# A list schedule of its own that pins the order of every engine's instructions in a two-layer encoder kernel

## The chip, the cores and the metric

The kernel runs as one program on one core of a Trainium2 chip. The metric is device time in microseconds (us), the median of three runs. A core has five engines that each take their instructions strictly in the order in which they were built: PE (matrix products), DVE (vector work), ACT (pointwise functions and casts), POOL (a second, slower vector engine) and SP (here the queue that issues all DMAs). An instruction waits on semaphores for what other engines must have done first, and everything behind it on its engine waits with it.

## The reference

Two layers over one sequence of 512 tokens, width 1024, 16 heads of 64, gated channel mixer of width 2816, all in float32:

```
layer 0: a = rmsnorm(h); q,k,v = split(a @ sb_w_qkv)
         o = stick_breaking_attention(q,k,v)     # sigmoid weights times a running product of (1-beta)
         h = h + rmsnorm(o @ sb_w_o)
         h = h + rmsnorm(conv_ffn(rmsnorm(h)))   # up, causal conv of width 3, gelu(gate)*up, down
layer 1: k,v,f from rmsnorm(h) @ w_kvf; q = rmsnorm(h) @ fox_w_q
         o = softmax(q k/8 + fcum[t] - fcum[s], causal) v
         h = h + rmsnorm(o @ fox_w_o)
         h = h + rmsnorm(conv_ffn(rmsnorm(h)))
```

## The kernel before

**Products.** Each float32 operand is split into a rounded part and a rest (hi and lo), and each product is made of three matmuls: hi·hi, hi·lo and lo·hi. Activations stand transposed in `AH`/`AL`; weights come as 192-odd tiles of 512 KB through a stream: `make` (L129) issues the DMA of a tile into `raw` (two buffers), casts it on ACT to `whi` (L144) and takes the rest on DVE to `wlo` (L148, two halves; three tiles of each output projection on POOL; with a gain folded in, L138/L139). `whi`/`wlo` have eight buffers each, so eight tiles at most are ahead of PE.

**Stages.** A stage `pre` (norm, transposes), `attn0` (16 heads of stick-breaking attention in eight pairs), `ffn0` (output projection, norm, up, down), `attn1` (16 heads of forgetting attention) and `ffn1`.

**A head** (`head`, L411). PE makes the scores of four query blocks (L419) into three PSUM banks. In layer 0: ACT exp (L452), DVE min and mask (L453, L429, L431), ACT ln (L455), DVE scan (L456), ACT exp (L457), DVE product (L458). In layer 1: DVE mask and maximum (L429, L431, L438), ACT exp of four blocks with row sums (L439), DVE reciprocal (L443), scaling of one block on DVE and three on POOL (L446). Then PE transposes the weights (L466), ACT and DVE split them (L472, L473), PE multiplies with V (L478), ACT and DVE take the result out (L487, L488). The next pair's projections (L213, L399) and, for the last heads, the output projection (L521) are what PE can do meanwhile.

**A transition** (`out_proj`, L530, and `mixed`, L576). For each of the four token blocks b the output projection runs over k = 0..7 (L521). Then `post_steps` and `pre_steps`: ACT square and sum (L250), POOL two small instructions for the root (L219, L220), DVE product with the gain and residual sum (L251, L253), again square (L230), root, scaling (L235), then PE transposes of that block (L238), ACT and DVE into `AH`/`AL` (L240, L241). The up projection of the first three chunks runs in two halves of 256 tokens (L605 to L609), so that its first half needs blocks 0 and 1 only.

**What sets the order.** The framework's scheduler orders each engine by a timeline of its own; `tc.high_priority()` marks the norm steps (L225, L245); `out_proj` writes the order of its 32 units out by hand, with `FILL` units between the last heads' parts, and ties each to the one before (`tc.issue_after`, L547); `down_proj` ties its last units the same way, and activation tables are loaded behind the users of the last one (L196).

Of the kernel before, what the change touches and what calls it, by code (L numbers as in the profile page):

```python
# [14 lines left out]
P = 128  # L15
# [13 lines left out]
EARLY = 3  # L29
POOL_ROWS = (1, 5, 7)  # L30
FILL = (4, 5)
# [6 lines left out]
def f32(ap):  # L38
    return ap.bitcast(F32)


@with_exitstack
def tile_trunk(
# [23 lines left out]

    const = ctx.enter_context(tc.tile_pool(name="const", bufs=1))
    small = ctx.enter_context(tc.tile_pool(name="small", bufs=4))
    wp = ctx.enter_context(tc.tile_pool(name="wp", bufs=1))  # L70
# [58 lines left out]
    def make(i):  # L129
# [5 lines left out]
        if g is not None:  # L135
            for k in range(nk):
                s = gcol[:, g + k : g + k + 1]
                nc.scalar.activation(hi[:, k], raw[:, k], AF.Copy, scale=s)  # L138
                nc.vector.scalar_tensor_tensor(  # L139
                    out=lo[:, k], in0=raw[:, k], scalar=s, in1=f32(hi[:, k]), op0=ALU.mult, op1=ALU.subtract  # L140
                )
            made[i] = (hi, lo)
# [48 lines left out]
    users = []  # L191

    def ins(i):
        return getattr(i, "ins", i)

    def act_table(name):  # L196
        with ExitStack() as stack:
            for i in users[-8:]:
                stack.enter_context(tc.issue_after(i))
            ld = nc.scalar.preload_act_table_set(name)  # L200
        return tc.issue_after(ins(ld))

    def uses_table(i):
        users.append(ins(i))
# [18 lines left out]
    def pre_block(b, g, t4, junk):  # L223

        with tc.high_priority():  # L225
            pre_steps(b, g, t4, junk)

    def pre_steps(b, g, t4, junk):
# [52 lines left out]
    class Attn:  # L281
# [128 lines left out]
        def head(self, p, hh):  # L410
# [22 lines left out]
            if fox:  # L433
                masked(z, mask_b, ALU.add)
                st = small.tile([P, 12], F32, name="st")
                for b in (3, 2, 0, 1):
                    sl = slice(ZOFF[b], ZOFF[b] + (b + 1) * P)
                    nc.vector.reduce_max(st[:, b : b + 1], z[:, sl], axis=AX.X, negate=True)  # L438
                    i = nc.scalar.activation(  # L439
                        E[:, sl], z[:, sl], AF.Exp, bias=st[:, b : b + 1], accum_out=st[:, 4 + b : 5 + b]  # L440
                    )
                    uses_table(i)
# [6 lines left out]
            else:  # L449
# [7 lines left out]
                uses_table(nc.scalar.activation(C, C, AF.Exp, scale=-1.0))  # L457
# [3 lines left out]
            for js in ((0,), (1, 3), (2,)):  # L461
                zt = bank("zt")
                o = 0
                for j in js:
                    for b in range(j, NB):
                        tr = nc.tensor.transpose(  # L466
# [22 lines left out]
            return ins(tr), ins(mm)  # L489

        def run(self):
# [7 lines left out]
            for p in range(NPAIR):  # L499
# [3 lines left out]
                end = self.head(p, 1)  # L503
# [7 lines left out]
            return end  # L511


    def unit(b, k, n, a, w, cols=(0, 1)):
# [4 lines left out]
        for i, (s, m) in enumerate(((ah, hi), (ah, lo), (al, hi))):  # L519
            for c in cols:  # L520
                mm = nc.tensor.matmul(  # L521
# [3 lines left out]
        return ins(mm)  # L525
# [4 lines left out]
    def out_proj(done, heads_end):  # L530

        w = {}
        after = []
        one = [(1, k) for k in range(KT)]
        order = [(0, k) for k in range(KT - 2)] + one[: FILL[0]] + [(0, KT - 2), heads_end[0]]
        order += one[FILL[0] : FILL[1]] + [heads_end[1]] + one[FILL[1] :]
        order += [(0, KT - 1)] + [(b, k) for b in (2, 3) for k in range(KT)]
        for step in order:
            if not isinstance(step, tuple):
                after.append(step)  # L540
                continue
            b, k = step
            if k not in w:
                w[k] = take()
            with ExitStack() as stack:
                for i in after:
                    stack.enter_context(tc.issue_after(i))  # L547
                after = [unit(b, k, KT, (AH[:, k, :], AL[:, k, :]), w[k])]
            if k == KT - 1:
                done(b)  # L550

    def down_proj(lhs, done, final, last=4):
        held = []
        for k in range(NC):
# [5 lines left out]
            for b in (0, 2, 3, 1):  # L560
                end = unit(b, k, NC, a, w)
        for b in range(NB):
            for cols in ((0,), (1,)) if final and b == NB - 1 else ((0, 1),):
                with tc.issue_after(end):
                    for k, a, w in held:
# [153 lines left out]
```

## Time and profile before

| | |
|---|---|
| median of 3 runs | 1271.66 us (1269.28 to 1274.44) |
| the profiled execution | 1273.83 us, span of its instructions 1272.1 us |
| PE / DVE / ACT / POOL busy | 97% / 64% / 51% / 8% of the span |
| instructions | 16,820 |

A busy PE is not PE at its best: matmuls overlap, so a row's mean duration (391 ns for 512 columns) is longer than the distance from one start to the next. Groups of instructions show busy time, mean duration of one, and the idle time just before them with what ended it; windows show each engine's busy time in a stretch, and the clock that PE was granted (1.00 is the upper of its two levels).

### The profile page before, as it was taken

Reading aid. Unit: us, or ns where it says so; the run is one execution under the profiler, and the core shown is the slowest. Engines: PE = TensorE matmul, PEld = TensorE weight load, DVE = VectorE, ACT = ScalarE, POOL = GpSimd, SP = SyncE. Lnnn points to the kernel's source line nnn. Section 1 sums busy time; section 2 is a strip of 40 time slices with the busy share of each in tenths; the row PEclk is TensorE's granted clock in tenths of the full one; section 3 lists DMA queues with packets and bytes.
Section 4 is the critical chain, followed back from the end, with each engine's and each line's share of the span. In section 5 each row is a group of like instructions: output and inputs, shape, how many; then the busy total and the mean of one; then the engine's idle time right before and its main releaser. Section 6 shows DMA issues by size and latency. Waiting matters only on the chain. (4 is left out here: it accounts for less than half of the span.)

```text
span 1272.1 us, 16820 instructions
## 1 busy us (share of the span) xinstructions
PE 1232.7 (97%) x6485; PEld 1060.8 (83%) x6485; DVE 811.1 (64%) x1304; ACT 644.6 (51%) x1085; POOL 102.0 (8%) x163
## 2 busy tenths in 40 slices
PE   6999998999999999999999999999999999999998
PEld 6888886789888888888888988978898888888886
DVE  6899898676655555433488887774775555554323
ACT  5767677445433333322488787663454333333221
POOL 1000003020000000000012213341100000000001
PEclk9999999999999999999999999999999999999999
DMA  7421212034333333233233122110543333322311
GB/s 218 136 66 51 67 50 67 23 94 138 111 99 99 97 92 95 98 99 100 67 83 86 53 81 67 58 43 33 149 118 99 99 99 100 97 91 94 99 34 66
DMA packets 145928, 111.97 MB, mean 88 GB/s; under 512 B 4680, under 2 KB 136120, under 8 KB 145848
## 3 DMA queue, kind: packets, MB, share of 16 engines
q1 hardware_dynamic: 145848, 110.90, 28.9%
q8 instruction: 51, 0.84, 0.3%
q14 instruction: 29, 0.24, 0.1%
HBM read 108.79 MB, written 2.10 MB: 87 GB/s over the span
## 5 line engine op out<-in xcount | busy, mean ns | idle before, releaser
L213 PE MATMUL PS<-AH,whi 128*128 128x512 f32 (+1 forms) x1088 | 398.1, 366 | 3.9 <-DVE QS L370 2.6
L213 PE MATMUL PS<-AL,whi 128*128 128x512 f32 (+1 forms) x1088 | 397.2, 365 | 0.0
L213 PE MATMUL PS<-AH,wlo 128*128 128x512 f32 (+1 forms) x1088 | 397.1, 365 | 0.0
L148 DVE TENSOR_TENSOR wlo<-raw,whi 128x512 fp32r<-128x512 f32 x332 | 217.4, 696 | 212.2 <-ACT whi L144 211.7
L144 ACT CAST whi<-raw 128x1024 fp32r<-128x1024 f32 x172 | 180.9, 1052 | 224.7 <-PE PS L213 178.5
L213 PEld LDWEIGHTS PS<-AH,whi 128*128 128x128 f32 x1088 | 205.5, 189 | 36.6 <-DVE QS L370 3.3
L213 PEld LDWEIGHTS PS<-AH,wlo 128*128 128x128 f32 x1088 | 205.3, 189 | 32.0
L213 PEld LDWEIGHTS PS<-AL,whi 128*128 128x128 f32 x1088 | 205.4, 189 | 31.3
L597 DVE SCALAR_TENSOR_TENSOR hc<-PS,cw,hc 128x511 f32<-128x511 f32 (+1 forms) x176 | 130.7, 745 | 2.7
L521 PE MATMUL PS<-whi,al 128*128 128x512 f32 x352 | 109.4, 389 | 0.0
L521 PE MATMUL PS<-wlo,ah 128*128 128x512 f32 x352 | 109.4, 389 | 0.0
L521 PE MATMUL PS<-whi,ah 128*128 128x512 f32 x352 | 109.3, 389 | 0.0
L620 DVE TENSOR_TENSOR al<-act,ah 128x512 fp32r<-128x512 f32 x44 | 30.4, 690 | 117.2 <-ACT ah L619 117.2
L619 ACT CAST ah<-act 128x512 fp32r<-128x512 f32 x44 | 27.4, 623 | 144.8 <-PE PS L521 138.3
L219 POOL TENSOR_SCALAR ss<-ss 128x1 f32<-128x1 f32 x31 | 12.0, 388 | 822.4 <-ACT junk L250 757.1
L399 PE MATMUL PS<-whi,AH 128*128 128x256 f32 x256 | 74.1, 290 | 3.9 <-DVE QS L370 1.6
L521 PEld LDWEIGHTS PS<-wlo,ah 128*128 128x128 f32 x352 | 66.1, 188 | 13.8
L521 PEld LDWEIGHTS PS<-whi,al 128*128 128x128 f32 x352 | 66.1, 188 | 13.7
L521 PEld LDWEIGHTS PS<-whi,ah 128*128 128x128 f32 x352 | 66.1, 188 | 13.6
L399 PE MATMUL PS<-wlo,AH 128*128 128x256 f32 x256 | 74.0, 289 | 0.0
L399 PE MATMUL PS<-whi,AL 128*128 128x256 f32 x256 | 73.6, 288 | 0.0
L602 ACT ACTIVATE hc<-hc 128x512 f32<-128x512 f32 x44 | 27.8, 631 | 86.4 <-DVE hc L597 86.4
(130 smaller groups left out, 1767.5 us busy)
## 6 DMA issues: line engine op xcount, KB each, us to landing
raw<-w_up_dram SPq DMA_DIRECT2D x88, 512.0 KB
raw<-w_down_dram SPq DMA_DIRECT2D x44, 512.0 KB
raw<-sb_w_qkv_dram SPq DMA_DIRECT2D x24, 512.0 KB
raw<-w_kvf_dram SPq DMA_DIRECT2D x16, 512.0 KB
raw<-sb_w_o_dram SPq DMA_DIRECT2D x8, 512.0 KB
raw<-fox_w_q_dram SPq DMA_DIRECT2D x8, 512.0 KB
raw<-fox_w_o_dram SPq DMA_DIRECT2D x8, 512.0 KB
H<-x_dram SPq DMA_DIRECT2D x4, 512.0 KB
```

What stands on the lines that cost most here:

```text
L144: nc.scalar.copy(hi, raw)
L148: eng.tensor_tensor(out=fl[:, s], in0=fr[:, s], in1=fh[:, s], op=ALU.subtract)
L213: nc.tensor.matmul(ps, a[:, k, :m], b[:, k, t0:t1], start=i == 0, stop=i == n - 1)
L219: nc.gpsimd.tensor_scalar(ss[:, 2:3], ss[:, 0:1], 1.0 / D, EPS, op0=ALU.mult, op1=ALU.add)
L399: nc.tensor.matmul(ps[:, o], a[:, k, sl], m[:, k % 4, :], start=i == 0, stop=i == 3 * KT - 1)
L521: mm = nc.tensor.matmul(y[:, c, :], s[:, sl], m[:, 0, c * 512 : (c + 1) * 512], start=k == 0 and i == 0, stop=k == n - 1 and i == 2,)
L597: nc.vector.scalar_tensor_tensor(out=hc[:, s:], in0=y[:, i, : T - s], scalar=col[:, 2 - s : 3 - s], in1=hc[:, s:], op0=ALU.mult, op1=ALU.add,)
L602: uses_table(nc.scalar.activation(hs[0], hs[0], AF.Gelu_apprx_tanh))
L619: nc.scalar.copy(ah, act[:, k, :])
L620: nc.vector.tensor_tensor(out=al, in0=act[:, k, :], in1=f32(ah), op=ALU.subtract)
```

## The change

The kernel records its instructions in program order, as before, and at the end `Order.pin` builds a dependency graph of the whole program (by 64-byte pieces of tiles, PSUM banks, tile buffers, activation tables), gives every instruction a cost by engine, operation and columns, and runs a list schedule: whichever engine is free first takes, among its instructions that are ready, the one of lowest rank. The rank is the place in the program, plus 300 for the split of a weight tile (`BEHIND`), minus 150 for an instruction other than PE's that reads or writes PSUM (`AHEAD`). The order that comes out is then tied on PE, DVE, ACT and POOL by a chain of dependencies from each instruction to the next. The hand-written order of `out_proj`, the high priorities, the ties of `down_proj` and of the table loads go. No instruction is added, removed or changed: 6,485 matmuls and 224 DMAs before and after. The order of the DMAs on SP is not pinned and differs in a few places.

```
+BEHIND = 300
+AHEAD = 150
-FILL = (4, 5)
+class Order:
+    ISSUE, FLIGHT, BYTES = 520, 2100, 200.0
+    HOP = 60
...
+    def cost(self, i):
...
+        if e == "PE":
+            return {512: 227, 384: 171, 256: 120}.get(n, max(109, 0.4427 * n)), 170 + 0.4427 * n
...
+        reads = [x for x in aps if self.columns(x) >= P]
+        narrow = len(reads) < len(aps)
+        n = max([n] + [self.columns(x) for x in reads])
+        if e == "DVE":
+            if n == ZLEN and op == "TensorScalarPtr" and len(reads) == 2:
+                d = 130 + 2.1 * n
+            elif len(reads) > 1 or any(x.bass_ap.tensor.name in self.banks for x in reads):
+                d = 155 + 1.04 * n + 65 * narrow
+            else:
+                d = 150 + 0.53 * n + 60 * narrow
+            return d - 80, d
+        if e == "Activation":
+            d = 135 + 0.9 * n + 150 * narrow + 60 * (len(i.outs) > 1)
+            return d + 20, d
+        if n < P:
+            d = 550 if op == "TensorTensor" else 190
+        else:
+            d = 200 + (2.3 if len(reads) > 1 else 1.3) * n
+        return d, d
...
+    def pin(self, psum, tables):
...
+        start = self.schedule(prog, preds)
+        by = {}
+        for n in sorted(range(N), key=lambda n: (start[n], n)):
+            by.setdefault(self.engine(prog[n]), []).append(prog[n])
+        info = mybir.DependencyInfo(mybir.DependencyClass.NoSync, mybir.DependencyReason.DATA)
+        for e, line in by.items():
+            if e != "SP":
+                for a, b in zip(line, line[1:]):
+                    self.tc.add_manual_dep(b, a.name, info)
+    def schedule(self, prog, preds):
+        N = len(prog)
+        rank = [n + self.shift.get(i.name, 0) - (AHEAD if self.evicts(i) else 0) for n, i in enumerate(prog)]
...
+            t, e = best
+            while later[e] and later[e][0][0] <= t:
+                m = heapq.heappop(later[e])[1]
+                heapq.heappush(now[e], (rank[m], m))
+            n = heapq.heappop(now[e])[1]
+            hold, done = cost[n]
+            start[n], free[e], end = t, t + hold, t + done
...
     def make(i):
-        nc.scalar.copy(hi, raw)
+        order.move(nc.scalar.copy(hi, raw), BEHIND)
...
-            eng.tensor_tensor(out=fl[:, s], in0=fr[:, s], in1=fh[:, s], op=ALU.subtract)
+            order.move(eng.tensor_tensor(out=fl[:, s], in0=fr[:, s], in1=fh[:, s], op=ALU.subtract), BEHIND)
...
-    def out_proj(done, heads_end):
-        order = [(0, k) for k in range(KT - 2)] + one[: FILL[0]] + [(0, KT - 2), heads_end[0]]
...
+    def out_proj(done):
+        w = {}
+        for b in range(NB):
+            for k in range(KT):
+                if k not in w:
+                    w[k] = take()
+                unit(b, k, KT, (AH[:, k, :], AL[:, k, :]), w[k])
+            done(b)
...
+    order.pin(PS, ("Exp", "Ln", "Gelu_apprx_tanh"))
```

What the pinned order is, at three places. The changed kernel's lines stand about 215 further down: its L380 and L384 are L144 and L148, L449 is L230, L454 is L235, L457 is L238, L459 is L240, L465 is L250, L670 is L456.

DVE in `attn0`, from the second half of the first keys' rest (`KL0`) to the first scan, before:

```order
L381 TENSOR_TENSOR KL0_237<-PS_67,KH_399 64x512
L148 TENSOR_TENSOR wlo11_575<-raw11_573,whi11_574 128x512 x2
L370 SCALAR_TENSOR_TENSOR QS_571<-PS_67,QS_571 64x512
L148 TENSOR_TENSOR wlo12_610<-raw12_608,whi12_609 128x512 x2
L370 SCALAR_TENSOR_TENSOR QS_571<-PS_67,QS_571 64x512
L453 TENSOR_SCALAR ec_528<-ec_528 128x1280
L429 TENSOR_TENSOR ec_528<-ec_528,mask_a_73 128x3x128
L431 TENSOR_TENSOR ec_528<-ec_528,mask_a_73 128x128
L148 TENSOR_TENSOR wlo13_751<-raw13_749,whi13_750 128x512 x2
L381 TENSOR_TENSOR KL1_238<-PS_67,KH_572 64x512
L456 SCALAR_TENSOR_TENSOR ec_529<-R_243,ec_529 128x1280
```

The same stretch on DVE in the changed kernel:

```order
L596 TENSOR_TENSOR KL0_237<-PS_67,KH_399 64x512
L384 TENSOR_TENSOR wlo7_274<-raw7_272,whi7_273 128x512 x2
L667 TENSOR_SCALAR ec_528<-ec_528 128x1280
L644 TENSOR_TENSOR ec_528<-ec_528,mask_a_73 128x3x128
L585 SCALAR_TENSOR_TENSOR QS_571<-PS_67,QS_571 64x512
L646 TENSOR_TENSOR ec_528<-ec_528,mask_a_73 128x128
L585 SCALAR_TENSOR_TENSOR QS_571<-PS_67,QS_571 64x512
L670 SCALAR_TENSOR_TENSOR ec_529<-R_243,ec_529 128x1280
```

Before, the splits of tiles up to 13 stand ahead of the first scan; now those up to 7 do, and the splits of six more tiles (`wlo8` to `wlo13`) come behind it.

ACT at the first transition (`ss_2386`, `ss_2414`, `ss_2484` are blocks 0, 1 and 2; a row with PS is a block's first square, one with H its second), before:

```order
L250 ACTIVATE junk_2238,ss_2386<-PS_67 128x1024
L230 ACTIVATE junk_2238,ss_2392<-H_81 128x1024
L250 ACTIVATE junk_2238,ss_2414<-PS_67 128x1024
L230 ACTIVATE junk_2238,ss_2420<-H_81 128x1024
L250 ACTIVATE junk_2238,ss_2484<-PS_67 128x1024
L240 CAST AH_82<-PS_67 128x8x128
```

The same on ACT in the changed kernel (`ss_2344` and `ss_2350` are block 0, `ss_2414` and `ss_2420` block 1):

```order
L465 ACTIVATE junk_2238,ss_2344<-PS_67 128x1024
L449 ACTIVATE junk_2238,ss_2350<-H_81 128x1024
L465 ACTIVATE junk_2238,ss_2414<-PS_67 128x1024
L380 CAST whi33_2266<-raw33_2265 128x1024
L380 CAST whi34_2279<-raw34_2278 128x1024
L459 CAST AH_82<-PS_67 128x8x128
L449 ACTIVATE junk_2238,ss_2420<-H_81 128x1024
```

Block 1's second square stood ahead of block 0's cast into `AH`; now it stands behind that cast and behind two weight casts.

PE at the same transition (`t4_2385` is block 0, `t4_2413` block 1), before; between the two transposes stand 22 matmuls of block 3's projection, of which the first three rows and the last are shown:

```order
L238 MATMUL PS_67<-ident_68,t4_2385 128x128 x8
L521 MATMUL PS_67<-whi24_1553,AH_82 128x512 x2
L521 MATMUL PS_67<-wlo24_1554,AH_82 128x512 x2
L521 MATMUL PS_67<-whi24_1553,AL_83 128x512 x2
...
L521 MATMUL PS_67<-wlo27_1820,AH_82 128x512 x2
L238 MATMUL PS_67<-ident_68,t4_2413 128x128 x8
```

The same on PE in the changed kernel (`t4_2343` is block 0, `t4_2413` block 1, `t4_2483` block 2; w31 is k = 7 of the output projection, w32 and w33 the first two tiles of the up projection):

```order
L733 MATMUL PS_67<-whi31_2240,AL_83 128x512 x2
L457 MATMUL PS_67<-ident_68,t4_2343 128x128 x8
L457 MATMUL PS_67<-ident_68,t4_2413 128x128 x8
L436 MATMUL PS_67<-AH_82,whi32_2253 128x256
L436 MATMUL PS_67<-AH_82,whi33_2266 128x256
L436 MATMUL PS_67<-AL_83,whi32_2253 128x256
L436 MATMUL PS_67<-AH_82,wlo32_2254 128x256
```

All four blocks' projections now stand ahead of the first transposes, and nothing stands between the transposes of blocks 0 and 1.

## Rows read from the trace of the kernel before

**Rows 1.** The page, its first part: busy time of each engine.
```profile
PE 1232.7 (97%) x6485; PEld 1060.8 (83%) x6485; DVE 811.1 (64%) x1304; ACT 644.6 (51%) x1085; POOL 102.0 (8%) x163
```
**Rows 2.** Chain that ended last, in time: start us, length us, engine and line.
```profile
915.53 230.74 PE PS L213 x1112
1146.27 119.69 PE PS L521 x528
```
**Rows 3.** Groups by shape on PE: count, busy us, mean ns, idle before.
```profile
L213 PE MATMUL PS<-AH,whi 128*128 128x512 f32 x832 | 325.4, 391 | 3.9 <-DVE QS L370 2.6 <-DVE V L405 1.3
...
L399 PE MATMUL PS<-whi,AH 128*128 128x256 f32 x256 | 74.1, 290 | 3.9 <-DVE QS L370 1.6 <-DVE AL L241 1.4 <-DVE KL L381 1.0
...
L521 PE MATMUL PS<-whi,AH 128*128 128x512 f32 x128 | 43.0, 414 | 4.4 <-DVE QS L370 3.0 <-ACT ec L439 1.5
```
**Rows 4.** Stretches: length, busy us of PE, PEld, DVE, ACT, POOL; clock, DMA.
```profile
56.00:210.00 154.00, 145.87 (x883) 129.56 (x882) 143.52 (x177) 114.55 (x155) 10.32 (x8) 0.99 0.20 61
60.00:90.00 30.00, 27.01 (x188) 24.56 (x186) 29.59 (x37) 22.52 (x30) 0.00 (x0) 1.00 0.19 53
210.00:250.00 40.00, 34.59 (x170) 28.76 (x168) 27.83 (x35) 21.56 (x33) 4.88 (x3) 0.91 0.06 17
250.00:300.00 50.00, 49.09 (x311) 44.26 (x310) 30.02 (x33) 21.31 (x29) 8.65 (x16) 1.00 0.38 117
640.00:660.00 20.00, 17.26 (x136) 16.41 (x135) 16.31 (x42) 17.76 (x46) 2.40 (x6) 1.00 0.40 109
660.00:835.00 175.00, 173.19 (x1086) 156.57 (x1085) 144.94 (x330) 138.05 (x359) 42.16 (x61) 1.00 0.24 70
835.00:875.00 40.00, 37.03 (x181) 30.29 (x180) 22.64 (x47) 20.76 (x50) 10.57 (x14) 0.91 0.05 14
900.00:920.00 20.00, 18.64 (x151) 18.10 (x150) 14.03 (x18) 10.18 (x12) 1.61 (x4) 1.00 0.59 175
```
**Rows 5.** Timeline of DVE, first scan and last head: start us, length us.
```profile
55.98 2.82 DVE L456 TENSOR_TENSOR_SCAN ec<-R,ec 128x1280 f32<-128x1280 bf16 x1 [0.36 <-ACT ec L455]
...
249.18 0.69 DVE L488 TENSOR_TENSOR oT<-PS,ot 64x512 f32<-64x512 f32 x1 [1.09 <-ACT ot L487]
```
**Rows 6.** Groups by shape on DVE: splits, residual sum, scaling, `AL`.
```profile
L148 DVE TENSOR_TENSOR wlo<-raw,whi 128x512 fp32r<-128x512 f32 x332 | 217.4, 696 | 212.2 <-ACT whi L144 211.7
...
L241 DVE TENSOR_TENSOR AL<-PS,AH 128x1024 fp32r<-128x1024 f32 x16 | 19.4, 1217 | 3.6 <-ACT AH L240 3.6
...
L235 DVE SCALAR_TENSOR_TENSOR t<-H,ss,g 128x1024 f32<-128x1024 f32 x12 | 15.4, 1283 | 17.8 <-POOL ss L220 17.8
```
**Rows 7.** Timeline of PE at the first transition: start us, length us.
```profile
264.74 1.03 PE L238 MATMUL PS<-ident,t 128*128 128x128 f32 x8
```
**Rows 8.** Groups by shape on ACT: exp with sums, square, `AH`.
```profile
L230 ACT ACTIVATE junk<-H 128x1024 bf16<-128x1024 f32 x16 | 16.9, 1056 | 28.1 <-DVE H L253 23.3 <-DMA H<-x_dram 4.8
L240 ACT CAST AH<-PS 128x1024 fp32r<-128x1024 f32 x16 | 16.1, 1004 | 1.5 <-PE PS L238 1.5
...
L439 ACT ACTIVATION_READ_ACCUMULATOR ec<-PS,st 128x1 f32 x64 | 13.1, 205 | 0.0
L439 ACT ACTIVATE ec<-PS,st 128x512 f32<-128x512 f32 x16 | 11.1, 691 | 1.7 <-DVE st L438 1.7
```
**Rows 9.** Timeline of POOL at the first transition: the root's two instructions.
```profile
259.45 0.19 POOL L219 TENSOR_SCALAR ss<-ss 128x1 f32<-128x1 f32 x1 [4.69 <-ACT junk L230]
259.73 0.55 POOL L220 TENSOR_TENSOR ss<-ss,mhalf 128x1 f32<-128x1 f32 x1
260.60 1.05 POOL L219 TENSOR_SCALAR ss<-ss 128x1 f32<-128x1 f32 x1 [0.32 <-ACT junk L250]
```
**Rows 10.** Timeline of DVE in the same stretch.
```profile
260.32 1.29 DVE L235 SCALAR_TENSOR_TENSOR t<-H,ss,g 128x1024 f32<-128x1024 f32 x1 [2.19 <-POOL ss L220]
```
**Rows 11.** Groups by shape on POOL: scaling of the weights' blocks.
```profile
L446 POOL TENSOR_SCALAR ec<-ec,st 128x384 f32<-128x384 f32 x16 | 12.9, 808 | 101.8 <-DVE st L443 92.5 <-PE PS L466 9.3
...
L446 POOL TENSOR_SCALAR ec<-ec,st 128x128 f32<-128x128 f32 x16 | 8.2, 514 | 0.0
```

More of the change, by code (lines that the diff above doesn't have):

```diff
@@ L1 @@
+import heapq
 from contextlib import ExitStack
@@ L66, in tile_trunk @@
     nc = tc.nc
+    order = Order(tc, ("pre", "attn0", "ffn0", "attn1", "ffn1"))
     const = ctx.enter_context(tc.tile_pool(name="const", bufs=1))
-    small = ctx.enter_context(tc.tile_pool(name="small", bufs=4))
-    wp = ctx.enter_context(tc.tile_pool(name="wp", bufs=1))
+    small = order.pool(ctx.enter_context(tc.tile_pool(name="small", bufs=4)), "small", 4)
+    wp = order.pool(ctx.enter_context(tc.tile_pool(name="wp", bufs=1)), "wp", 1)
     psum = ctx.enter_context(tc.tile_pool(name="psum", bufs=1, space=bass.MemoryType.PSUM))
@@ L188, in tile_trunk @@
     stream += ffn_stream(1)
[L191 to L204, printed above, removed]
+    act_table = nc.scalar.preload_act_table_set
     def w_stationary(ps, w, t0=0, t1=T, m=P):
@@ L502, in run @@
                     self.project(p + 1)
-                end = self.head(p, 1)
+                self.head(p, 1)
                 if p % 2 and p + 1 < NPAIR:
@@ L560, in down_proj, with ffn_phase @@
             for b in (0, 2, 3, 1):
-                end = unit(b, k, NC, a, w)
+                unit(b, k, NC, a, w)
         for b in range(NB):
             for cols in ((0,), (1,)) if final and b == NB - 1 else ((0, 1),):
-                with tc.issue_after(end):
-                    for k, a, w in held:
-                        end2 = unit(b, k, NC, a, w, cols)
-                end = end2
+                for k, a, w in held:
+                    unit(b, k, NC, a, w, cols)
             done(b)
-    def ffn_phase(l, heads_end, post_g, next_g, final):
+    def ffn_phase(l, post_g, next_g, final):
         with tc.tile_pool(name=f"ffn{l}", bufs=2) as pool:
+            pool = order.pool(pool, f"ffn{l}", 2)
             g1 = gain(pool, post_g)
@@ L683, in tile_trunk @@
     with tc.tile_pool(name="attn0", bufs=2) as pool:
-        with act_table("natural_log_exp_and_others"):
-            end = Attn(pool, False).run()
-    ffn_phase(0, end, sb_post_g[0], None, False)
+        pool = order.pool(pool, "attn0", 2)
+        act_table("natural_log_exp_and_others")
+        Attn(pool, False).run()
+    ffn_phase(0, sb_post_g[0], None, False)
     with tc.tile_pool(name="attn1", bufs=2) as pool:
-        with act_table("natural_log_exp_and_others"):
-            end = Attn(pool, True).run()
-    ffn_phase(1, end, fox_post_g[0], None, True)
+        pool = order.pool(pool, "attn1", 2)
+        act_table("natural_log_exp_and_others")
+        Attn(pool, True).run()
+    ffn_phase(1, fox_post_g[0], None, True)
+    order.pin(PS, ("Exp", "Ln", "Gelu_apprx_tanh"))
 _INS = [
```

228 lines of the change are left out of this document (183 added, 45 removed).

## The prediction

> **What bounds the kernel now.** I read the page first: PE is busy for 1232.7 us [rows 1] of a span of 1272.1, so 39.4 us of idle time is what any new order can win, beside stretches at the lower clock. Then the chain of waits: from 915.53 to the end it is PE alone, 230.74 us of up projection and 119.69 us of 528 down-projection matmuls, with no wait in it [rows 2]. The second is PE's pace, 119.69 / 528 = 0.227 us for 512 columns; the mean of 0.391 in the groups [rows 3] overlaps. The layer-0 channel mixer runs in the same way. So the order can gain in `attn0`, in `attn1` and at the transitions only. The groups of PE say whom it waits for there: its projections wait for DVE's `QS`, `V` and `KL`, which take PSUM out, the output projection for `QS` and ACT's exp [rows 3].
>
> The windows give the places [rows 4]. In `attn0` DVE is the busiest engine beside PE: 143.52 of 154 us from 56 to 210, and 29.59 of 30 us (1.4% idle) from 60 to 90. From 210 to 250, where no projections are left, PE is busy for 34.59 of 40 us and its clock is 0.91: between full and half speed (2.4 and 1.2 GHz) that is 7.2 us at half speed, 3.6 us of work lost. The end of `attn1`, 835 to 875, has 2.97 us of idle time and the same clock; its middle, 660 to 835, has only 1.8 us of idle time; 640 to 660, the entry, has 2.7. The transitions cost little before: 0.9 us from 250 to 300 and 1.4 from 900 to 920.
>
> **The heads of layer 0.** Their stretch on DVE goes from the first scan at 55.98 to the last head's result, which ends at 249.87 [rows 5]: 193.9 us, of which 143.52 + 27.83 = 171.4 busy [rows 4] and 22.5 idle (11.7%). The change moves twelve halves of weight splits (`wlo8` to `wlo13`) and the half `KL1` from ahead of the first scan to behind it, as the order of DVE shows. One split takes 0.696 us [rows 6]; instructions of DVE overlap a little, so I take 0.64. The first scan then comes up to 12 x 0.64 = 7.7 us earlier, 48.3 at best; but it also needs its own scores from PE, and those come about 4 us earlier only (18 matmuls fewer ahead of them at 0.227), 52. I take 50. Behind it DVE now has 171.4 + 13 x 0.64 = 179.7 us to do. If it never idled, the heads would end at 229.7. What idle time stays is not in the trace; its bounds are the best window's 1.4% (2.5 us) and the 11.7% of the whole stretch before (24 us). I take 6 us, nearer to the first: the idle time lies mostly in 210 to 250 (12.2 us), where heads had no splits or projections beside them, and splits that give way are the filler that this stretch lacked. The heads then end at 235.7, 14.2 earlier. PE has also done more by then: counted in the two orders, 12 more matmuls of 512 columns stand ahead of the last head's value product, 2.7 us. Sum: -16.9 (bounds -20.5 and +1).
>
> PE can follow: counted in the new order, its work ahead of that product is about 211 us by its pace, well below 235.
>
> **Transition 0.** Here the order gets worse. Before, 22 matmuls of 512 columns stood between the transposes of blocks 0 and 1 (5 us), which hid block 1's norm. Now all projections are done before block 0's transposes, and nothing stands between. On ACT, block 1's second square stands behind two weight casts and behind block 0's cast into `AH`, which itself waits for block 0's transposes. So block 1's path starts only with these: transposes 1.03 [rows 7], then `AH` 1.0, square 1.06, its read 0.2 as that of an exp [rows 8], POOL's root 0.19 + 0.55 [rows 9], scaling on DVE 1.28 [rows 6]: 5.3 us. From POOL to DVE the hand-off took 0.04 (0.55 behind 259.73, and 260.32) [rows 9, 10], from ACT over POOL's two instructions more; I allow 0.4 for all, an estimate. PE is busy for the first 1.03 and stands for 4.7 us. Then it does block 1's transposes and waits again, for block 1's `AH` 1.0 and `AL` 1.2 [rows 6, 8] (2.6 with hand-offs and what ACT and DVE still have from other blocks). 7.3 us of idle time, and one stretch at half clock behind it: a 40 us window with 5.4 us of idle time lost 3.6 us in two such stretches [rows 4], so one is 1.8. Less the 0.9 that this place cost before: +8.2, bounds +5.5 (no clock loss, weight casts or up products found to fill in) and +10.
>
> POOL's root may cost more: at 260.60 its first instruction took 1.05 us instead of the 0.19 at 259.45 [rows 9], just while DVE ran a scaling with two inputs, 260.32 to 261.61 [rows 10]. The Trainium skill has this as a rule (SBUF — State Buffer, Who interferes with whom): such a DVE instruction holds a port pair that GpSimd shares, and the one that comes second waits for it. The trace agrees here. By the rule each block whose root meets another block's scaling pays about 0.9 us.
>
> **Transition 1.** Ten matmuls of 512 columns (2.3 us) now stand between the transposes of blocks 0 and 1, in the same pattern otherwise: 4.7 - 2.3 = 2.4, then 2.6 for block 1's casts, and 1.8 if the clock falls, less the 1.4 of before. I take +4.5, bounds +2 and +6.
>
> **Entry of layer 1.** 2.7 us idle [rows 4]. The new order has work of `ffn0`'s last units in front of what waits here; I take -2 (bounds -3 and 0).
>
> **The heads of layer 1.** Here the new order is tighter: by its rows and PE's pace, PE mostly has 0.9 to 1.6 us of other work between a head's transposes and its value product, where it often had 4 to 6 before. The schedule believes its costs. They can be held against the trace. Its formula for ACT gives 0.806 us for an exp of 512 columns with a row sum (135 + 0.9 x 512 + 150 + 60 ns); the trace has 0.691 + 0.205 = 0.896 [rows 8], 0.09 more and some 0.35 over a head's four. On POOL 699 ns stand for 384 columns where the trace has 808, and 366 for 128 where it has 514 [rows 11]: 0.26 together. With 0.1 for hand-offs that the formula's even 0.06 may undercount, an estimate, a head's chain is 0.7 us longer than planned, 11 us over 16 heads. Two heads alternate, and half of the slips should be swallowed by the other head's work: +5.5. Against it stand the middle's idle time of before, -1.8, and the end's: 2.97 + 3.6 = 6.6, of which I take 4 off, since the output projection now spreads freely between the last heads. Sum 0, bounds -6 and +10.
>
> **The rest** is costed at 0. In both channel mixers PE's chain has no wait [rows 2] and a split that waits 300 places is hidden by the tiles ahead, eight buffers of them; if that cover fails, a late split costs its 0.7 us once. The start and the tail do the same steps.
>
> **Sum** against the profiled 1273.8: -16.9 + 8.2 + 4.5 - 2 + 0 = -6.2, 1267.6. The profiled execution lies 2.2 us above the median of the runs, 1271.7; 1265.4 on that scale, and I forecast 1265.
>
> **Rivals.**
> *DVE keeps the idle share of its long window.* 56 to 210 has 6.8% [rows 4], with splits there to fill in; on 179.7 us that is 12 instead of 6, and the time is 1271. For it: scan, logarithm and product of a head go back and forth between ACT and DVE whatever stands between. Against it: the 1.4% of 60 to 90.
>
> *Layer 1 slips at every head (the slower side).* The places before a value product have no slack, so each of the 16 heads pays its 0.7 us in full, 11 instead of 5.5; the gain at the end of these heads (4) does not come, since the last two have nothing beside them; and the stops bring two more half-clock stretches (3.6). 1265 + 5.5 + 4 + 3.6 = 1278, and 1280 with both transitions near their upper bounds. It decides as soon as more than two thirds of the heads pay in full. For it: pinned, no engine can take anything else when one instruction is late. Against it: before, PE was idle for 1% of 660 to 835, so slack is not short on average. What the skill says of the shared port (page and section as above) would add to it wherever a split on DVE, which has two inputs, meets POOL's scaling.
>
> *Layer 0's heads end no earlier.* If idle time stays at 11.7%, the first term is +1 instead of -16.9: 1283. For it: the last two heads are one serial chain in any order.
>
> *All goes well.* DVE at 1.4% idle (-3.5), transitions at their lower bounds (-5), no slip in layer 1 (-3): 1254.
>
> **How the numbers follow.** The forecast has 0.43, with a range of its own of 1256 to 1272; the first rival 0.20, the second 0.18, the third 0.06, the last 0.13. Half a per cent, 6.4 us, is about what can be told from no change: faster is below 1265.3, slower above 1278.0. Faster: 0.28 of the forecast's 0.43, the good case's 0.13 and 0.02 of the first rival, 0.43. Slower: 0.15 of the second, 0.06 of the third and 0.02 of the first, 0.23. The same: 0.34. Leaving out a tenth on each side the range is 1251 to 1283.
>
> **What would show it.** In the windows of the changed kernel: the first scan on DVE near 50 us, DVE idle for 3 to 4% from there, the last head's result near 236. At transition 0 two PE stops of some 4.7 and 2.6 us, each ended by DVE (scaling, then `AL`), with a clock below 1 behind them; if PE shows no stop over 2 us there, that term is wrong. In layer 1 many waits of PE of half a microsecond ended by POOL's scaling or ACT's exp; if the windows from 660 to 835 stay 99% busy, no slip exists. The forecast as a whole is wrong if the heads of layer 0 end after 245, or if layer 1 needs over 10 us more or less than before.

## The result, and the profile after

The changed kernel takes 1281.14 us (median of 5 runs, 1280.78 to 1283.62) where the kernel before takes 1272.02 beside it (5 runs): a ratio of 1.0073, 95% interval 1.0048 to 1.0098. It is slower by 9 us; the forecast was 1265. The profiled execution took 1283.62 us, the slowest of its five, against 1273.83 before.

The page's busy times, changed kernel; the instructions are the same, PE has 7.9 us more and its span is 1281.8:

```profile
PE 1240.6 (97%) x6485; PEld 1061.9 (83%) x6485; DVE 812.4 (63%) x1304; ACT 649.4 (51%) x1085; POOL 103.5 (8%) x163
```

The same stretches as in [rows 4], changed kernel, and ahead of them the first 20 us (columns: stretch, length, busy us of PE, PEld, DVE, ACT, POOL, clock, DMA share, GB/s):

```profile
0.00:20.00 20.00, 7.73 (x36) 6.71 (x37) 8.26 (x17) 8.60 (x12) 3.17 (x15) 1.00 0.63 215
56.00:210.00 154.00, 152.49 (x924) 133.71 (x923) 149.73 (x193) 120.99 (x168) 12.64 (x8) 1.00 0.25 76
60.00:90.00 30.00, 29.98 (x201) 26.86 (x200) 29.53 (x39) 22.84 (x33) 0.00 (x0) 1.00 0.21 60
210.00:250.00 40.00, 37.21 (x176) 30.94 (x175) 27.67 (x32) 21.79 (x27) 2.53 (x2) 0.91 0.11 34
250.00:300.00 50.00, 43.07 (x255) 38.68 (x254) 28.48 (x31) 20.76 (x28) 9.14 (x16) 0.90 0.33 97
640.00:660.00 20.00, 20.00 (x150) 19.01 (x149) 14.67 (x31) 17.26 (x40) 2.97 (x9) 1.00 0.13 30
660.00:835.00 175.00, 170.93 (x1059) 152.25 (x1058) 142.99 (x333) 136.79 (x355) 32.81 (x52) 0.99 0.22 63
835.00:875.00 40.00, 37.57 (x190) 29.35 (x189) 27.24 (x54) 27.93 (x61) 17.09 (x20) 1.00 0.24 72
900.00:920.00 20.00, 15.39 (x91) 13.66 (x90) 17.66 (x19) 12.05 (x17) 7.91 (x12) 0.83 0.25 80
```

The first 20 us of the kernel before:

```profile
0.00:20.00 20.00, 10.13 (x61) 9.13 (x62) 12.09 (x23) 11.22 (x15) 5.30 (x18) 1.00 0.75 241
```

Better than in [rows 4] are 56 to 210 (PE idle 1.5 us instead of 8.1), 210 to 250 (2.8 instead of 5.4), 640 to 660, and the clock from 835 to 875. Worse are the start, where PE does 36 matmuls instead of 61, both transitions, 250 to 300 (6.9 us idle instead of 0.9, clock 0.90 instead of 1.00) and 900 to 920 (4.6 instead of 1.4, clock 0.83), and 660 to 835 (4.1 instead of 1.8).

Windows are cut at fixed times, and the work in them shifts. So I also counted lost PE time by stage. For each matmul of PE's timeline I took the distance from its start to the next one's, less its pace at full clock (227 ns for 512 columns, 172 for 384, 120 for 256, 60 for 128, 109 for a transpose). All 6,485 paces sum to 1206.8 us, the same in every run here. What remains is idle time and half-clock time together (us, profiled executions; the start ends with the first score matmul, the heads of a layer with its last value product; the runs from e_sp on are explained with the experiments):

| run | start | layer 0 heads | transition 0 | layer 1 entry and heads | transition 1 | sum | profiled time |
|---|---|---|---|---|---|---|---|
| before | 5.0 | 26.5 | 1.3 | 17.4 | 1.6 | 51.8 | 1273.8 |
| changed | 8.8 | 15.4 | 11.4 | 17.6 | 8.3 | 61.5 | 1283.6 |
| e_sp | 9.2 | 17.1 | 0.3 | 20.3 | 0.5 | 47.4 | 1269.1 |
| e_bytes | 7.2 | 17.2 | 10.8 | 21.2 | 8.5 | 64.9 | 1286.5 |
| e_both | 8.2 | 20.2 | 1.5 | 22.9 | 1.2 | 54.0 | 1276.0 |
| e_behind0 | 9.5 | 14.9 | 14.2 | 24.0 | 11.9 | 74.5 | 1296.2 |
| e_start | 5.1 | 15.3 | 11.4 | 17.7 | 8.2 | 57.7 | 1279.8 |
| e_l0none | 8.8 | 28.8 | 0.3 | 20.5 | 0.5 | 58.9 | 1281.0 |
| e_h90 | 9.4 | 14.1 | 11.1 | 20.3 | 9.1 | 64.0 | 1285.6 |
| e_sp_start_a75 | 5.5 | 19.5 | 0.5 | 21.4 | 0.5 | 47.4 | 1269.2 |
| e_sp_start_a75_h90 | 5.5 | 16.9 | 0.4 | 17.9 | 0.1 | 40.8 | 1262.6 |
| e_sp_start_h90 | 5.7 | 16.1 | 0.4 | 20.3 | 0.1 | 42.6 | 1264.5 |
| e_a75_h30 | 5.5 | 18.8 | 1.2 | 19.6 | 1.5 | 46.6 | 1268.5 |
| e_a75_h160 | 5.7 | 17.8 | 0.1 | 19.1 | 0.0 | 42.7 | 1264.2 |

The channel mixers lose nothing in any run. Profiled time less sum lies between 1221.5 and 1222.1 in all 14 rows, so these five places account for every difference. From before to changed: +3.8, -11.1, +10.1, +0.2, +6.7, together +9.7; the two profiled times differ by 9.8. Idle time of PE is only 1.8 us of it (41.2 us instead of 39.4); for the rest PE was busy longer, and most of that is the lower clock: in the stretches with a granted clock of 0.50, the last 6 us of the span left out, PE was busy for 23.8 us instead of 13.4.

**Transition 0.** PE of the changed kernel (start us, length us; in brackets the idle time and who ended it):

```profile
268.91 1.06 PE L457 MATMUL PS<-ident,t 128*128 128x128 f32 x8 [0.46 <-DVE t L454]
...
274.87 1.97 PE L457 MATMUL PS<-ident,t 128*128 128x128 f32 x8 [4.90 <-DVE t L454]
...
277.94 0.79 PE L436 MATMUL PS<-AH,whi 128*128 128x256 f32 x2 [1.10 <-ACT AH L459]
...
279.20 0.58 PE L436 MATMUL PS<-AL,whi 128*128 128x256 f32 x1 [0.47 <-DVE AL L460]
```

The 4.90 is the forecast stop for block 1's scaling. Block 1's transposes behind it last 1.97, where those of block 0, and those in [rows 7], take about 1.05: they ran at the lower clock, granted from 274.24 on. Why does nothing stand between the two transposes? PE's order of the changed kernel, where the projections end (`whi_2240`, `wlo_2241` are w31, the tile of k = 7; `whi_1819` is that of k = 3):

```
L733 MATMUL PS<-whi_1819,AH 128x512 x2
L733 MATMUL PS<-wlo_1820,AH 128x512
L733 MATMUL PS<-whi_2240,AH 128x512 x6
L733 MATMUL PS<-wlo_2241,AH 128x512
L733 MATMUL PS<-whi_2240,AL 128x512
```

Six matmuls of w31 in a row are those of blocks 0, 1 and 2 with two halves each: all three blocks end their projection together, and as late as w31. What is then left of block 3, 27 matmuls or 6 us, covers block 0's norm alone. Where that tile was, ACT of the changed kernel tells (its cast, and block 0's first square):

```profile
245.83 1.05 ACT L380 CAST whi<-raw 128x1024 fp32r<-128x1024 f32 x1
...
261.51 1.02 ACT L465 ACTIVATE junk<-PS 128x1024 bf16<-128x1024 f32 x1 [5.57 <-PE PS L733]
```

And its DMAs on SP (start us, time of the issuing):

```profile
195.83 6.54 SPq L369 DMA_DIRECT2D raw<-sb_w_o_dram  x2
214.34 0.38 SPq L369 DMA_DIRECT2D raw<-w_up_dram  x1
246.73 0.33 SPq L492 DMA_DIRECT2D g<-sb_post_g_dram  x1
```

The second DMA of the first row is w31, whose issuing ends at 195.83 + 6.54 = 202.37, and such a tile takes 3.5 to 3.6 us from issue to landing in this stretch. Its data lay in `raw` from about 206, and the pinned ACT cast it at 245.83, 40 us later. What held it was the plan, not the chip: `pin()` ties all DMAs into one chain in program order in its own picture, and there w31 comes behind the gain tiles `g` of the channel mixer, which must wait until `attn0` releases their memory. On the chip SP is not pinned; the framework's order issues w31 at 202 and the gains at 246.73. The plan has its cast at 248 of its own time, so it gave PE all units k = 0 to 6 of blocks 0, 1 and 2, and the first ones of block 3, ahead of w31.

**The start.** ACT of the kernel before, and then of the changed one:

```profile
8.03 1.06 ACT L230 ACTIVATE junk<-H 128x1024 bf16<-128x1024 f32 x1 [1.89 <-DMA H<-x_dram]
...
10.43 1.01 ACT L240 CAST AH<-PS 128x1024 fp32r<-128x1024 f32 x1
```

```profile
10.44 1.01 ACT L459 CAST AH<-PS 128x1024 fp32r<-128x1024 f32 x1 [4.29 <-PE PS L457]
11.35 1.06 ACT L449 ACTIVATE junk<-H 128x1024 bf16<-128x1024 f32 x1
```

Block 1's tokens had landed by 8.03 and its square began at once. In the changed kernel the square stands behind block 0's cast, ACT sits idle until 10.44, and the square starts 3.32 us later. Block 1's transposes on PE follow it, at 14.79 instead of 11.47. The plan's rate of 200 bytes per ns (`BYTES`) lets these tokens come too late. PE loses 8.8 us here instead of 5.0.

### The profile page after: what moved, and what is told of

It is laid out like the page before. It is cut to its first block, busy times and chain, and to the rows that moved or that the text cites. A ratio compares the mean times of both kernels' runs of the same rounds, so it can differ in the third digit from the quotient of the medians.

```text
span 1281.8 us, 16749 instructions
## 1 busy us (share of the span) xinstructions
PE 1240.6 (97%) x6485; PEld 1061.9 (83%) x6485; DVE 812.4 (63%) x1304; ACT 649.4 (51%) x1085; POOL 103.5 (8%) x163
## 4 chain that ended last, share of the span: by engine, by line
PE 86%; DVE 9%; ACT 2%; issue 2%; POOL 0%; DVEq 0%; POOLq 0%; ACTq 0%
PE PS L436 49%; PE PS L733 23%; PE PS L614 6%; PE PS L692 3%; PE PS L680 2%; PE PS L634 2%; DVE ec L670 1%; PE PS L457 1%; DVE wlo L384 1%; DVE PL L687 1%; DVE ec L672 1%; DVE t L454 1%; DVE QS L585 1%; DVE t L466 0%; DVE ec L667 0%
## 5 line engine op out<-in xcount | busy, mean ns | idle before, releaser
L384 DVE TENSOR_TENSOR wlo<-raw,whi 128x512 fp32r<-128x512 f32 x332 | 216.7, 690 | 211.4 <-ACT whi L380 210.9
L380 ACT CAST whi<-raw 128x1024 fp32r<-128x1024 f32 x172 | 180.1, 1050 | 197.5 <-PE PS L436 167.4
L792 ACT ACTIVATE hc<-PS,cw 128x512 f32<-128x512 f32 x88 | 68.1, 774 | 8.4 <-PE PS L436 8.3
```

The costliest lines, as they stand in the source:

```text
L380: order.move(nc.scalar.copy(hi, raw), BEHIND)
L384: order.move(eng.tensor_tensor(out=fl[:, s], in0=fr[:, s], in1=fh[:, s], op=ALU.subtract), BEHIND)
L792: nc.scalar.activation(hc, y[:, i, :], AF.Identity, scale=col[:, 2:3], bias=col[:, 3:4])
```

## The experiments

My theory (A in the expectations): the loss is in the planner's picture of the DMAs, at the transitions the chain through the gain tiles and at the start the slow load; the list schedule itself is good. Among the rivals is that the plan's hand-offs are too short, so that its lists are too tight everywhere (C).

**e_sp, the queue alone.** The gain tiles are left out of the plan's chain:

```diff
-            if str(i.opcode) == "DMACopy":
+            if str(i.opcode) == "DMACopy" and not (wr and wr[0].bass_ap.tensor.name.startswith("g_")):
```

> The planner's DMA queue is changed alone: the gain tiles of a mixer (g) no longer hold back the weight DMAs behind them in its model, as they do not on the chip, where the last weight tile of the output projection was issued some 40 us ahead of them. Theory A (the planner believes the last tile late, so PE's pinned order does all units of k = 0 to 6 of all four blocks first and nothing is left between the transposes): both transitions fall to about what they cost before, 11.4 to 2 us and 8.2 to 2.5 us of lost PE time, some 13 to 15 us together; 1281 becomes 1266 to 1270. Theory B (a greedy list schedule spends the projection's units under the last heads' waits whatever it believes of the DMA): the stops stay, 1278 to 1281. Theory C (tight orders slip against real durations, the transitions only show it): at most 3 us, 1278.

Measured: 1269.82, ratio 0.9982 (0.9972 to 0.9992). ACT of this run now casts two tiles in a row, w31 among them, at 211.19, and block 0's first square starts 12 us earlier than in the changed kernel:

```profile
211.19 1.99 ACT L380 CAST whi<-raw 128x1024 fp32r<-128x1024 f32 x2
...
249.46 1.02 ACT L465 ACTIVATE junk<-PS 128x1024 bf16<-128x1024 f32 x1 [1.95 <-PE PS L733]
```

Its PE has blocks 0, 1 and 2 six microseconds apart, with projections between and no wait:

```profile
258.96 1.03 PE L457 MATMUL PS<-ident,t 128*128 128x128 f32 x8
...
264.84 1.04 PE L457 MATMUL PS<-ident,t 128*128 128x128 f32 x8
...
270.75 1.03 PE L457 MATMUL PS<-ident,t 128*128 128x128 f32 x8
```

The window from 250 to 300, and the one ahead of it:

```profile
210.00:250.00 40.00, 35.26 (x169) 29.33 (x168) 29.79 (x32) 22.10 (x28) 3.15 (x2) 0.91 0.11 32
250.00:300.00 50.00, 49.99 (x341) 46.13 (x340) 33.29 (x38) 23.59 (x33) 7.60 (x16) 1.00 0.37 113
```

The transitions lose 0.3 and 0.5 us instead of 11.4 and 8.3: 18.9 us back. Of these, 4.8 are given back: heads of both layers lose more (17.1 for 15.4, 20.3 for 17.6), most of it in the last heads, whose gaps the projections had filled (35.26 busy from 210 to 250, where the changed kernel has 37.21), and 0.4 is lost at the start. One line turns slower into slightly faster, within the time that theory A gave; theory A holds for the transitions.

**e_bytes and e_both, the load rate** (e_both has the line of e_sp as well):

```diff
-    ISSUE, FLIGHT, BYTES = 520, 2100, 200.0
+    ISSUE, FLIGHT, BYTES = 520, 2100, 350.0
```

> The planner's DMA rate is raised from 200 to 350 bytes per ns, nothing else; the traces show 300 to 410 GB/s while the first tiles flow. Theory A (planner's picture of the DMA): block 1's square no longer stands behind block 0's cast into AH at the start, which gives back the 3 to 4 us lost there; the output projection's last tile is believed some 3 us earlier but still behind the gains, so the transitions give back 1 to 3 us; 1274 to 1278. Theory B2 (the start is lost because the first weight casts give way by 300 places): the start stays as it is, 1280 to 1281.

> Both edits of the planner's DMA model together (gains do not hold back weights, 350 bytes per ns). Theory A: the gains add, 16 to 19 us off 1281, 1262 to 1266, below the 1272 of the kernel before. Theory B (greedy order): 1274 to 1278, no better than the kernel before. Theory C (slips): 1275.

Measured: 1285.23, ratio 1.0105 (1.0088 to 1.0121), and 1274.18, 1.0018 (1.0003 to 1.0032). Both miss what theory A gave. The time of e_both is the one that the rivals B and C gave, but its transitions lose 1.5 and 1.2 us and not the stops of B. For a tile of 512 KB the plan now counts 2.1 + 1.5 = 3.6 us, the 3.5 to 3.6 seen above, instead of 4.7. The start gets 1.6 us better, but a faster rate for every load puts weight casts earlier on ACT than their data is there, and what stands behind the cast waits too. ACT of e_both just ahead of layer 0's first scores:

```profile
42.46 1.04 ACT L380 CAST whi<-raw 128x1024 fp32r<-128x1024 f32 x1 [2.77 <-DMA raw<-sb_w_qkv_dram]
43.53 0.58 ACT L594 CAST KH<-PS 64x512 fp32r<-64x512 f32 x1
44.12 0.58 ACT L595 CAST KH<-PS 64x512 fp32r<-64x512 f32 x1
```

Its PE waited for these keys (in e_bytes the same wait is 1.5 us):

```profile
44.75 0.61 PE L634 MATMUL PS<-KH,QS 128*128 128x512 f32 x2 [2.40 <-ACT KH L595]
```

Up to 20 us PE loses 4.8 us in e_both, near the 4.6 of before the change and not the changed kernel's 7.5; this wait, which still falls into the column of the start, takes most of that back. So the slow rate is wrong for the first loads, and for the later ones it leaves a margin. In e_bytes layer 0's heads lose 1.8 us more than in the changed kernel and layer 1 3.6; in e_both 3.1 and 2.6 more than in e_sp. Whether that comes from such waits is not shown, since every list is drawn anew.

**e_start, the load rate of the first 5 us alone:**

```diff
-                wire = max(wire, t + 1300) + done - self.FLIGHT
+                wire = max(wire, t + 1300) + (done - self.FLIGHT) * (0.57 if t < 5000 else 1)
```

> The changed kernel, with the planner's DMA rate raised (by 1/0.57, to 350 bytes per ns) for the DMAs that it issues in its first 5 us alone: the token blocks, the first gain, the first two weight tiles. Theory A (the start is lost because the plan takes block 1's tokens for late and puts its square behind block 0's cast into AH): the square goes back to 8 us as before, 3 us of PE time return at the start and nothing else moves but by chance (up to 3 us either way): 1276 to 1281, most likely 1278. Theory A2 (e_bytes lost 4 us because a rate near the true one leaves no margin, and ACT then stands in its pinned order before weight casts whose tile has not landed, with PSUM takes behind it): no such wait of 1 to 3 us of ACT ahead of a K cast at 40 to 45 us here, unlike with 350 for all. Rival (any re-roll of the list costs 4 us by chance): 1283 to 1286.

Measured: 1279.05, ratio 1.0055 (1.004 to 1.007). The square of block 1 is ahead of the cast again, on ACT of this run, and the start loses 5.1 us, as before the change; all else stays within 0.1 of the changed kernel. ACT has no wait for a weight tile ahead of the keys' casts at 40 to 45 us. The profiled executions differ by 3.8 us, the medians by 2.1 only, as the changed kernel's profiled execution is its slowest:

```profile
7.78 1.06 ACT L449 ACTIVATE junk<-H 128x1024 bf16<-128x1024 f32 x1 [1.61 <-DMA H<-x_dram]
...
10.46 1.01 ACT L459 CAST AH<-PS 128x1024 fp32r<-128x1024 f32 x1 [1.53 <-PE PS L457]
```

**e_behind0, no shift for the weight splits:**

```diff
-BEHIND = 300
+BEHIND = 0
```

> The changed kernel with BEHIND = 0: weight splits keep their place in the program, all else as it is. If the splits that give way are what won 11 us in the heads of layer 0, the time rises by about as much, to 1288 to 1292, and DVE's idle time from the first scan to the last head's result goes up again. If instead they cost the start its 4 us and win nothing, it falls to 1277.

Measured: 1293.83, ratio 1.0168 (1.0149 to 1.0187). The time is 1.8 us above what was expected, and the place is another: layer 0's heads lose 14.9, no more than with the shift, and DVE idles for 12.2 us from the first scan to the last head's result, where the changed kernel has 12.6; the transitions lose 2.8 and 3.6 more and layer 1 6.4. What the forecast gave as cause of the gain in the heads, splits that give way, isn't it by itself.

**e_l0none, no shift of either kind up to the end of layer 0's attention**, with the line of e_sp (place 1857 of the program is the end of that stage):

```diff
-        rank = [n + self.shift.get(i.name, 0) - (AHEAD if self.evicts(i) else 0) for n, i in enumerate(prog)]
+        rank = [n + (self.shift.get(i.name, 0) - (AHEAD if self.evicts(i) else 0) if n > 1857 else 0) for n, i in enumerate(prog)]
```

> On the kernel with the mended queue (e_sp, 1269.8): no rank shift, neither BEHIND nor AHEAD, for the instructions up to the end of layer 0's heads; the rest as it is. If one of the two rules is enough to keep the scores' chain moving (BEHIND = 0 alone left the heads' loss at 14.9 us), taking both away brings back what the kernel before lost there: 17 goes to 23 to 27 us, and the time to 1276 to 1280. If the gain in the heads is the list schedule's own, whatever the ranks, the heads stay at 15 to 18 us and the time at 1268 to 1272.

Measured: 1282.09, ratio 1.0082 (1.0067 to 1.0097), slower than either theory gave. The heads lose 28.8, as much as before the change (26.5) and 11.7 more than e_sp. In the middle of layer 0, e_sp has a full PE at full clock and this kernel hasn't; first e_sp, then e_l0none:

```profile
60.00:100.00 40.00, 39.97 (x256) 35.51 (x255) 39.36 (x53) 29.79 (x43) 0.00 (x0) 1.00 0.23 67
```

```profile
60.00:100.00 40.00, 35.37 (x204) 30.56 (x203) 36.13 (x48) 28.59 (x37) 0.00 (x0) 0.91 0.28 84
```

So the gain in the heads comes from the shifts: with that of the instructions on PSUM alone it stays (e_behind0), without both it is gone. Whether the splits' alone would do was not tried.

**The corrections together, and the hand-off.** e_sp_start_a75 has the lines of e_sp and e_start and `AHEAD = 75`; e_sp_start_a75_h90 has `HOP = 90` besides (the plan's time from one engine to another, 60 ns); e_sp_start_h90 keeps `AHEAD = 150`; e_a75_h30 and e_a75_h160 are the first with `HOP` 30 and 160; e_h90 is the changed kernel with `HOP = 90` alone:

```diff
-AHEAD = 150
+AHEAD = 75
-    HOP = 60
+    HOP = 90
```

> Both edits of the planner's DMA model, queue (e_sp) and the first 5 us (e_start), and AHEAD = 75 in place of 150, so that PSUM takes pass fewer other instructions. Theory A: the gains of queue and start add, 1269.8 - 3 = 1267; with AHEAD halved the two stops of PE at the gates of layer 1 (4.3 us at 676 to 684 in e_sp, ended by QS) shrink by 2 to 3 us if they come from takes of other heads' projections that pass the gates' chain: 1263 to 1266. If the stops stay, 1266 to 1269. Rival C (tight orders slip): the heads of layer 1 stay at 20 us, 1268 or more.

> The same with a planned hand-off of 90 ns in place of 60 (the traces have 33 from ACT to DVE, 54 to PE, 93 from DVE to ACT, 86 to 165 to POOL). Theory C (orders that are planned too tight slip at every head): the loss in both layers' heads falls by 3 to 5 us together, 1259 to 1263. If the slips are hidden by the other head's work, it changes only by chance, 1262 to 1268.

> The changed kernel with one edit, a planned hand-off of 90 ns in place of 60. Theory C (orders planned with too short hand-offs slip at every head, and this is part of the loss of 10 us): heads of layer 0 15.4 to 13, heads of layer 1 17.6 to 14, time 1275 to 1277. Theory A (the planner's picture of the DMA is the loss, hand-offs are noise): 1279 to 1283, both transitions as they are (11 and 8 us).

> Mended queue and first DMAs, AHEAD = 150 as in the change, hand-off 90. If the 5 us between the last two kernels (1267.6 and 1262.5) are the hand-off's, this one has them too, 1261 to 1264; if they were a lucky list, 1264 to 1269. The two stops at the gates of layer 1 tell whether AHEAD moves them: 4.3 us with 150, 3.8 to 4.3 with 75.

> Mended queue and first DMAs, AHEAD = 75, hand-off 30 in place of 60: tighter still. Theory C: the heads of both layers lose 2 to 5 us more than with 60 (19.5 and 21.4), 1269 to 1273. Chance: 1263 to 1269.

> The same with hand-off 160, the longest that the traces show. Theory C: the heads lose as little as with 90 or less, 1259 to 1263. If 90 was a lucky list: 1263 to 1269.

| run | median | ratio to before |
|---|---|---|
| e_sp_start_a75 | 1267.56 | 0.9960 (0.9942 to 0.9978) |
| e_sp_start_a75_h90 | 1262.48 | 0.9930 (0.9915 to 0.9944) |
| e_h90 | 1286.18 | 1.0119 (1.0102 to 1.0137) |
| e_sp_start_h90 | 1263.94 | 0.9942 (0.9927 to 0.9956) |
| e_a75_h30 | 1270.29 | 0.9985 (0.9975 to 0.9996) |
| e_a75_h160 | 1264.55 | 0.9947 (0.9932 to 0.9962) |

With `AHEAD = 75` the medians over `HOP` 30, 60, 90, 160 read 1270.3, 1267.6, 1262.5, 1264.6, which looks like theory C, and e_sp_start_h90 lies in the range that stood for the hand-off. But theory C is about the heads, and what the two layers' heads lose together is 38.4, 40.9, 34.8 and 36.9 in this series: with 30 less than with 60, where C gave 2 to 5 us more. The run with 160 lies in the range that stood for chance. On the changed kernel 90 makes the median 5 us slower (the profiled executions differ by 2), above both theories' ranges. A new number draws every list anew, and that alone moves a stage by some us (layer 1 loses between 17.9 and 21.4 over these runs, with no order in it). Whether a longer hand-off helps by itself stays open, and so does what `AHEAD = 75` does: no run has both corrections with 150 and a hand-off of 60. The two stops of PE at layer 1's first head, which 75 was to shorten by 2 to 3 us, come to 3.9 us in e_sp and in e_sp_start_h90 and to 2.4 to 3.9 in the four runs with 75.

What holds in all five runs that have both corrections is the start at 5.5 to 5.7 and the transitions at 0.0 to 1.5. The best version, e_sp_start_a75_h90, beats the kernel before by 0.7% and, by the medians, the changed one by 1.5%. Its windows at the start, the end of layer 0's heads and the transitions:

```profile
0.00:20.00 20.00, 10.43 (x61) 9.66 (x61) 11.00 (x19) 10.08 (x14) 5.96 (x18) 1.00 0.75 241
210.00:250.00 40.00, 35.97 (x171) 29.29 (x170) 28.16 (x29) 19.86 (x26) 4.24 (x4) 0.96 0.13 38
250.00:300.00 50.00, 49.99 (x356) 46.76 (x355) 35.95 (x43) 26.62 (x36) 7.49 (x14) 1.00 0.36 108
875.00:920.00 45.00, 45.00 (x321) 42.22 (x321) 31.77 (x37) 21.31 (x28) 6.13 (x12) 1.00 0.40 115
```

## Why the prediction was wrong

The sum was -6.2, and +9.7 came, 15.9 more: 5.8 of it in layer 0's heads, 3.8 at the start, 1.9 and 2.2 at the transitions and 2.2 in layer 1 with its entry. Term by term:

**"The rest is costed at 0 ... The start and the tail do the same steps": the step that failed in kind.** The steps are the same, their order on ACT is not, and 3.8 us were lost there. e_start undoes just that and gets 3.7 back. The order alone could have shown it: the square of block 1 moves behind the `AH` cast on ACT, the same pattern that the prediction priced at transition 0. An order has to be read from its first row.

**Layer 0 heads, -16.9 forecast, -11.1 measured.** The largest miss in size, inside its bounds; the step that failed is the 6 us of idle time on DVE. The first scan and the last head's result, DVE of the changed kernel:

```profile
54.82 2.83 DVE L670 TENSOR_TENSOR_SCAN ec<-R,ec 128x1280 f32<-128x1280 bf16 x1 [0.61 <-ACT ec L669]
...
244.58 0.69 DVE L702 TENSOR_TENSOR oT<-PS,ot 64x512 f32<-64x512 f32 x1 [1.22 <-ACT ot L701]
```

The first scan is at 54.82 and not at 50: it came 1.2 us earlier than in [rows 5], with 3.8 us lost at the start in it. From there to 245.27 are 190.45 us, in which DVE was busy for 177.88 (the sum said 179.7): 12.6 us idle, not 6. That is the first rival's amount, 6.6%, but not its shape. From 56 to 210 DVE idles for 2.8% only. From 210 to the end of the heads, first in the changed kernel and then before, it idles for 8.3 of 35.3 us (23%) and for 12.0 of 39.9 (30%):

```profile
210.00:245.27 35.27, 32.48 (x155) 27.04 (x154) 26.98 (x31) 20.22 (x25) 0.00 (x0) 0.90 0.06 16
```

```profile
210.00:249.87 39.87, 34.46 (x169) 28.68 (x167) 27.83 (x35) 21.47 (x32) 4.88 (x3) 0.91 0.06 17
```

The splits that give way were to fill this stretch, and they did not: DVE has no more work in it than before, 27.0 us and 27.8. Whether another order could fill it is not shown. The heads end at 245.27, just behind the 245 that the prediction had named as its sign of being wrong.

**Transition 0, +8.2 forecast, +10.1 measured; transition 1, +4.5 and +6.7.** The mechanism was right; the term that was too small is the lower clock. PE's idle time is near the forecast: 6.9 us where the sum had 7.3 (the first stop 4.90, forecast 4.7; the second 1.10 and 0.47), and 4.6 where it had 5.0. But the granted clock stayed at half longer; transition 0 and then transition 1 of the changed kernel:

```profile
274.24:284.48 10.24, 8.04 (x34) 7.35 (x35) 9.45 (x10) 4.11 (x6) 3.85 (x6) 0.50 0.42 118
...
909.12:915.94 6.82, 6.14 (x27) 5.84 (x28) 6.27 (x8) 3.20 (x5) 3.16 (x4) 0.50 0.30 94
```

At half clock half of PE's 8.04 and 6.14 us is lost, an estimate of 4.0 and 3.1 us, where the sum took 1.8 for each, from two stretches of 3.4 us of the kernel before. Both amounts are slightly above the upper bounds (10 and 6). At transition 1 the prediction's own terms also add up to 5.4, and it took 4.5 without a reason. What the prediction did not ask is why the plan leaves nothing there. The answer, a tile that the plan thinks is late, would have said that the loss is an error of the model and not a price of the change.

On the shared port the prediction cited the Trainium skill (SBUF — State Buffer, Who interferes with whom). The trace agrees again: a root's first instruction on POOL took 1.05 us at 267.76 instead of 0.19, while DVE's scaling ran from 267.48. It cost nothing here, since DVE was busy until 269.90 with the product that its next step also needs.

**Entry of layer 1, -2; heads of layer 1, 0; measured +0.2 together.** The entry is full (640 to 660), but its stop has only moved to the first head, PE of the changed kernel:

```profile
692.94 0.50 PE L436 MATMUL PS<-AH,whi 128*128 128x512 f32 x1 [3.08 <-DVE QS L585]
```

The entry and that head lose 0.0 + 6.6 us, where they lost 3.2 + 2.7. Of the other heads, the second to the twelfth lose 4.5 instead of 2.6 and the last four 6.4 instead of 8.8, with a clock of 1.00 instead of 0.91 from 835 to 875. So there is a slip, but of 1.9 us and not 5.5, let alone the second rival's 11, and hardly any of it is idle time: of the 4.1 us from 660 to 835, 3.9 belong to the first head. The end gains 2.4 us of the 4 that were taken; in e_sp, where the projection no longer waits for w31, the last four heads lose 10.5. The -1.8 for the middle is wrong in sign: that idle time was the first head's stop, and it grew. The sum near nothing was right by luck, of terms that were all off.

**The rivals.** The time fell near the second rival's 1280 and the third one's 1283, inside the stated range of 1251 to 1283, for neither one's reason. "Slower" had 0.23, and none of it stood for an error in the plan's picture of DMAs, though the prediction did hold the plan's costs for ACT and POOL against the trace. Those were off by 0.09 to 0.15 us each; what was off by 40 us at one tile was when the data comes.

## What to carry to other kernels

A pinned order is as good as the planner's picture of what it doesn't pin: hold the plan's arrival time of each load against the trace first, and only then its costs. In a pinned order look for an instruction whose data has long landed and which stands behind a wait (here a square 3.3 us and a cast 40 us late), at the program's first rows too. A pessimistic load time can be a margin for an engine that works in order (with a faster one a cast stood 2.77 us for its tile), so mend it where it misleads; and as any new number draws all lists anew, compare stages, not totals.

## What the runs showed of the hardware

DVE, too, took longer beside POOL. DVE of e_both, the two masks of one head and a later scan:

```profile
194.94 1.62 DVE L644 TENSOR_TENSOR ec<-ec,mask_a 128x384 f32<-128x384 f32 x1
...
196.48 1.36 DVE L646 TENSOR_TENSOR ec<-ec,mask_a 128x128 f32<-128x128 f32 x1
...
217.78 3.90 DVE L670 TENSOR_TENSOR_SCAN ec<-R,ec 128x1280 f32<-128x1280 bf16 x1
```

POOL in the same stretches, splits of weight tiles with two inputs:

```profile
194.85 2.85 POOL L384 TENSOR_TENSOR wlo<-raw,whi 128x512 fp32r<-128x512 f32 x2 [28.93 <-ACT whi L380]
...
215.95 3.05 POOL L384 TENSOR_TENSOR wlo<-raw,whi 128x512 fp32r<-128x512 f32 x2 [3.80 <-PE PS L634]
```

The medians of these three in the same run are 0.559, 0.285 and 2.821 us, so each took 1.06 to 1.08 us longer, less than one of POOL's two instructions lasts (2.85 and 3.05 us for two). It doesn't explain the result: such overtime on DVE, counted where it is over 0.25 us above the median of its shape, sums to 6.8 us before, 4.6 in the changed kernel and 7.6 in e_sp.
